# Regrouping the levels of a chunked scan inside a two-mixer encoder layer

## The chip, the cores and the metric

The kernel runs on one core of a Trainium2 chip. The metric is the device time of one execution in microseconds. Before the change three runs gave 1809.49, 1810.12 and 1810.22 us; the median is 1810.12.

## The reference: what is computed

One encoder layer over 1024 positions of width 1024, in float32. A normalised input is projected once onto 8192 columns, and two mixers run on them. The first is a convolution module. The second, which the change concerns, is a gated linear recurrence in both directions with 8 heads of width 128:

```python
a = jnp.cumsum(lfb, axis=2)
diff = a[:, :, :, None, :] - a[:, :, None, :, :]
decay = jnp.where(tril, jnp.exp(jnp.minimum(diff, 0.0)), 0.0)
scores = jnp.einsum("bhtk,bhsk,bhtsk->bhts", qb, kb, decay)
o = (jnp.einsum("bhts,bhsv->bhtv", scores, vb)
     + jnp.einsum("bhtk,bhkv->bhtv", qb * jnp.exp(a), state))
```

A score between positions t and s is a sum over key channels in which each channel is damped by the product of the forget gates that lie between s and t. The two directions are summed, normalised per head, gated by a third projection and projected back. The gated sum of both mixers goes through an output projection and a residual, and a gated feed-forward block with a short convolution and a last normalisation follow.

## The kernel before, in words

Large products are made from float32 values split into a rounded high part and a remainder, so that one product is three matmuls (`mm3`, lines 147 to 149: `mm<-hx,wp` in the profile). ScalarE rounds, VectorE subtracts (`split`, line 123). These are the dense work. It is cut into units by `yield`; most units are two steps of k, six matmuls of 512 columns. `Stream.fill(n)` runs n units and carries fractions over.

TensorE's instructions keep the order in which the program writes them. The other engines are ordered by a planner, which may bring an instruction forward as soon as its inputs and its buffer are there. A tile's buffers rotate: a new one waits until the last reader of the old one is done. In PSUM the scan uses `sc` (2 banks), `tr` (2) and `ob` (1); `mm` (3) belongs to the dense work.

The scan works through 16 half heads: 8 heads, each in two halves of 512 positions. One half head has four chunks of 128 positions. The damping within a chunk is not formed as a product over pairs of positions. Instead the scan doubles a block size h = 1, 2, 4, ... 64: at level h the scores between two neighbouring blocks of h positions are one product of keys, damped to the edge between the blocks, and queries, damped from it. After each level `double` (line 1111, its products on line 1052) multiplies keys `kG`, queries `qF` and block totals `tb` by the totals of the neighbours, so that they fit the next level.

- `scan_inputs` loads queries and gates and forms keys and forget factors on ScalarE, with a clip on VectorE.
- `scan_base` makes the diagonal (line 1138, two products per block, one for each direction) and levels 1, 2 and 4 in one `sc` bank, in 5 steps. Each level is 16 matmuls of 128 rows by 32 columns, four per chunk, that sit in different column groups of the array (`level`, line 1103). Their stationary operand is a page `A`, into which `key_blocks` (ScalarE, line 1083) has copied the keys so that the keys of a left and a right block stand side by side; the moving operand is a strided view of `qF`. Masks then pick the valid scores of each level into `D` (line 1153).
- `scan_levels` does levels 8 and 16 in the same way, each with an `ob` bank of its own (masks on lines 1187 and 1189), then 32 and 64 as plain blocks (`blocks`, line 1167) in an `sc` bank that is first zeroed by a matmul of zeros `none` (line 1182). It ends by copying everything to `S`.
- `scan_states` transposes the keys through two `tr` banks (line 1203), copies them (`kT`, line 1205) and multiplies them with the values (line 1212; `ob` for one direction, `sc` for the other). VectorE chains the forward states `Sf` out of `ob` (line 1220).
- `outputs` (with `scan_outputs`), one head later: it chains the backward states, then makes the output of each half in `ob` (line 1253), copies and squares it on ScalarE (1255, 1258), normalises it (1272), and turns each half back through a `tr` bank (1279), out of which VectorE reads (1281).

These parts are woven by `between`, called at every `yield` of `scan_levels` and `scan_states`. One call is a *place*: `FILL` = 1.3 units of dense work, one step of the next half head's base, and one step of the previous head's outputs (`pending`). There are 4 places from the levels and 3 from the states, 7 per half head and 14 per head; 7 x 1.3 = 9.1 units per half head. The base has 5 steps, the outputs have 8.

In one half head TensorE thus meets, each with dense work ahead of it: level 8; level 16; the next base's diagonal and level 1, then `none`, blocks of 32 and the transpose of the values (line 1353); level 2 and blocks of 64; level 4 and one key transpose; the other key transpose; the state products. The first base is made ahead of the loop, with 6 units and then 3 units after each of its steps.

Of the kernel before, what the change touches and what calls it, by code (L numbers as in the profile page):

```python
# [10 lines left out]
F32 = mybir.dt.float32  # L11
# [35 lines left out]
def tile_hybrid_encoder(  # L47
# [54 lines left out]
    def page(pool, tag, bufs, dt=F32):  # L102
        return pool.tile([P, H], dt, tag=tag, name=nm(tag), bufs=bufs)
# [973 lines left out]
    def pairs(t, h, other=H):  # L1077

        return view(t, 0, [[other + h, 2], [2 * h, H // (2 * h)], [1, h]])

    def key_blocks(kG, h):
        A_t = page(hp, "A", 3)
        A.copy(pairs(A_t, h, 0), pairs(kG, h))  # L1083
        return A_t

    def slot(b, n):
        return b[:, n * P : (n + 1) * P]
# [7 lines left out]
    def each():  # L1095
        for c in range(4):
            for g in range(0, P, 32):
                yield c * P + g, slice(g, g + 32), slice(32 * c, 32 * c + 32)

    def level(b, A_t, qF, h):  # L1100

        for at, g, o in each():
            T.matmul(  # L1103
                b[g, o].rearrange("p (b x e) -> p b x e", x=2, e=h),
                A_t[:, at : at + 32],
                view(qF, at, [[2 * h, 16 // h], [H + h, 2], [1, h]]),
                start=True,
                stop=True,
            )

    def double(kG, qF, tb, h, to=None):
# [3 lines left out]
        tt(pairs(qF, h), pairs(qF, h), view(tb, nb + 1, [[-(nb + 1), 2], [2, n], [0, h]]))  # L1115
        if to is None:
            tn = hp.tile([P, 2, n], F32, tag=f"tb{h}", name=nm("tb"), bufs=2)
            to = view(tn, 0, [[n, 2], [1, n]])
        else:
            tn = None  # L1120
        tt(to, view(tb, 0, [[nb, 2], [2, n]]), view(tb, 1, [[nb, 2], [2, n]]))
        return tn

    def scan_base(ins):


        q, f, kG, ks = ins
        qF = hp.tile([P, 2, H], F32, tag="qF", name=nm("qF"), bufs=4)
        D_t = hp.tile([P, 4, 32], F32, tag="D", name=nm("D"), bufs=3)
        for d in range(2):  # L1130
            V.tensor_scalar(kG[:, d, :], kG[:, d, :], ks[:, d : d + 1], None, op0=ALU.mult)
        A_t = key_blocks(kG, 1)
        tt(qF, view(q, 0, [[0, 2], [1, H]]), view(f, H, [[-H, 2], [1, H]]))
        yield
        b = bank("sc")
        for at, g, o in each():
            for d in range(2):
                T.matmul(
                    slot(b, 3)[g, o],
                    kG[:, d, at : at + 32],  # L1140
                    q[:, at : at + 32],
                    start=d == 0,
                    stop=d == 1,
                )
        tb = f
        for n, h in enumerate((1, 2, 4)):
            level(slot(b, n), A_t, qF, h)
            tb = double(kG, qF, tb, h)
            A_t = key_blocks(kG, 2 * h)
            yield  # L1150
        A.copy(D_t, near(slot(b, 2)))
        for n, m in ((0, m_1), (1, m_2), (3, m_d)):
            V.copy_predicated(D_t, over(m), near(slot(b, n)))
        yield qF, kG, A_t, tb, D_t

    def scan_levels(base, S_t, Tt):


        qF, kG, A_t, tb, D_t = base

        def blocks(b, h):

            for c in range(0, H, P):
                for s0 in range(0, P, h):
                    t0 = s0 ^ h
                    d = s0 // h % 2
                    T.matmul(  # L1167
                        b[s0 : s0 + h, c + t0 : c + t0 + h],
                        kG[:, d, c + s0 : c + s0 + h],
                        qF[:, 1 - d, c + t0 : c + t0 + h],  # L1170
                        start=True,
                        stop=True,
                    )

        for h in (8, 16, 32, 64):
            if h < 32:
                b = bank("ob")
                level(slot(b, 0), A_t, qF, h)
            else:
                if h == 32:  # L1180
                    b = bank("sc")
                    T.matmul(b, none[:, :P], none, start=True, stop=True)
                blocks(b, h)
            tb = double(kG, qF, tb, h, view(Tt, 0, [[4, 2], [1, 4]]) if h == 64 else None)
            if h == 8:
                A_t = key_blocks(kG, 16)
                V.copy_predicated(D_t, over(m_8), near(slot(b, 0)))
            elif h == 16:
                V.copy_predicated(D_t, over(m_16), near(slot(b, 0)))
            elif h == 64:  # L1190
                A.copy(S_t, c4(b))
                for g in range(0, P, 32):
                    A.copy(S_t[g : g + 32, :, g : g + 32], D_t[g : g + 32])
            yield

    def scan_states(i, kG, v, Tt, Sf, Sb):

        half = i % 2
        kTs = []
        for d in range(2):  # L1200
            b = bank("tr")
            for c in range(4):
                T.transpose(b[:, c * P : (c + 1) * P], kG[:, d, c * P : (c + 1) * P], ident)
            kT = page(hp, "kT", 2)
            A.copy(kT, b)
            kTs.append(kT)
            yield
        for d in range(2):
            u = bank("sc" if d else "ob")
            for c in range(4):  # L1210
                sl = slice(c * P, (c + 1) * P)
                T.matmul(u[:, sl], kTs[d][:, sl], v[:, c, :], start=True, stop=True)
            u4 = c4(u)
            if d == 0:
                for c in range(4 if half == 0 else 3):
                    nx = Sf[half][:, c + 1, :] if c < 3 else Sf[1][:, 0, :]
                    if half == 0 and c == 0:
                        V.tensor_copy(nx, u4[:, 0, :])
                    else:
                        V.scalar_tensor_tensor(  # L1220
                            nx,
                            Sf[half][:, c, :],
                            Tt[:, half, 0, c : c + 1],
                            u4[:, c, :],
                            op0=ALU.mult,
                            op1=ALU.add,
                        )
# [102 lines left out]
    for h in range(NH):  # L1330
        Tt = hp.tile([P, 2, 2, 4], F32, tag="Tt", name=nm("Tt"), bufs=3)
        Sf = [hp.tile([P, 4, DK], F32, tag="st", name=nm("Sf"), bufs=4) for _ in range(2)]
        Sb = [hp.tile([P, 4, DK], F32, tag="st", name=nm("Sb"), bufs=4) for _ in range(2)]
        kept = []
        for half in range(2):
            i = 2 * h + half
            base = cur.result()
            ahead = Base(ins) if i + 1 < NI else None
            ins = scan_inputs(i + 2) if i + 2 < NI else None

            def between(fill):
                dense.fill(fill)
                if ahead is not None:
                    ahead.step(BASE_STEPS)
                pending.fill(1)

            S_t = hp.tile([P, 4, P], F32, tag="S", name=nm("S"), bufs=3)
            vl = load(d_v[h][half])
            for n, _ in enumerate(scan_levels(base, S_t, Tt[:, half])):
                if n == 2:  # L1350
                    b = bank("tr")
                    for c in range(4):
                        T.transpose(b[:, c * P : (c + 1) * P], vl[:, c * P : (c + 1) * P], ident)
# [407 lines left out]
```

## Time and profile before

| | |
|---|---|
| median of 3 runs | 1810.12 us |
| profiled execution | 1807.26 us, span 1805.5 us |
| TensorE busy | 1757.3 us, 97% |
| VectorE busy | 1213.0 us, 67% |
| ScalarE busy | 804.1 us, 45% |
| granted TensorE clock, mean | 0.993 |

In the profile PE is TensorE's matmuls and PEld its weight loads, DVE is VectorE, ACT ScalarE, POOL GpSimd. A group's row has line, engine, operation, output and inputs by the program's names, shapes and count; behind the first bar the busy time and the mean duration of one in nanoseconds; behind the second the idle time of the engine just ahead of the group and what ended it. A float32 matmul that is written once in the code leaves two records, except for transposes. A row of waits has the waiting instruction, what released it, the sum in microseconds, how often, and the longest. In rows in order of time the columns are start and duration in microseconds, then engine, line, operation, names, shapes and the count that was merged into the row.

### The profile page before, as it was taken

What the parts mean: (1) busy time and instruction counts of PE and PEld (TensorE: products, weight loads), DVE (VectorE), ACT (ScalarE), POOL (GpSimd) and SP (SyncE); (2) the same over time, 40 slices, a digit from 0 to 9 for tenths busy, and PEclk for the clock granted to TensorE, in tenths of its full rate; (3) what the DMA queues carried; (4) which work ended last, traced back from release to release, by engine and by line L of the source; (5) the groups of instructions that cost most, each with busy time, mean ns of one, the idle gap of its engine ahead of it and who ended that gap; (6) DMA issues with size and microseconds to landing.
All of it is one profiled execution on the core that took longest, in us unless ns stands there. A gap on an engine that the chain in (4) does not pass through costs nothing.

```text
span 1805.5 us, 30702 instructions
## 1 busy us (share of the span) xinstructions
PE 1757.3 (97%) x12150; PEld 1433.9 (79%) x12150; DVE 1213.0 (67%) x1813; ACT 804.1 (45%) x1534; POOL 152.2 (8%) x165
## 2 busy tenths in 40 slices
PE   8989999999999999999989999999999999999997
PEld 6878877888877778877878888878888888888885
DVE  4599999657577777777545666766766766545355
ACT  6344332335466566756552245434434434422123
POOL 1201111000000000000000002011111111000000
PEclk9999999999999999999999999999999999999999
DMA  8658878746652333335358666576776765534233
GB/s 279 215 153 187 190 174 187 203 146 199 209 177 95 120 107 117 118 101 177 112 171 236 200 205 207 142 152 144 147 158 147 151 152 129 161 97 128 82 93 135
DMA packets 321270, 284.48 MB, mean 158 GB/s; under 512 B 14942, under 2 KB 242022, under 8 KB 321126
## 3 DMA queue, kind: packets, MB, share of 16 engines
q1 hardware_dynamic: 279958, 250.01, 44.0%
q0 software_dynamic: 41168, 32.51, 12.8%
q8 instruction: 95, 1.56, 0.3%
q14 instruction: 49, 0.40, 0.1%
HBM read 189.40 MB, written 76.81 MB: 147 GB/s over the span
## 4 chain that ended last, share of the span: by engine, by line
PE 72%; DVE 9%; DMA 7%; ACT 5%; issue 4%; POOL 1%; SPq 1%; POOLq 0%; ACTq 0%; DVEq 0%
PE mm L147 17%; PE mm L149 16%; PE mm L148 16%; PE sc L147 3%; PE sc L149 3%; PE sc L148 3%; DVE acc L956 2%; PE ob L1253 2%; DVE wp L123 2%; PE tr L147 2%; PE tr L149 2%; PE tr L148 2%; DMA ev<-d_ga 1%; PE sc L1103 1%; DMA wr<-in_w_in_dram 1%
## 5 line engine op out<-in xcount | busy, mean ns | idle before, releaser
L147 PE MATMUL mm<-hx,wp 128*128 128x512 f32 x1144 | 463.0, 405 | 9.3 <-DVE ev L718 4.9
L149 PE MATMUL mm<-hx,wp 128*128 128x512 f32 x1144 | 449.9, 393 | 2.1 <-DVE wp L123 2.0
L148 PE MATMUL mm<-hx,wp 128*128 128x512 f32 x1144 | 449.0, 392 | 0.0
L123 ACT CAST wp<-wr 128x1024 fp32r<-128x1024 f32 (+2 forms) x171 | 162.0, 948 | 342.9 <-PE mm L148 258.3
L147 PEld LDWEIGHTS mm<-hx,wp 128*128 128x128 f32 x1144 | 216.6, 189 | 56.1 <-DVE ev L718 7.4
L149 PEld LDWEIGHTS mm<-hx,wp 128*128 128x128 f32 x1144 | 216.3, 189 | 50.6 <-DVE wp L123 3.8
L148 PEld LDWEIGHTS mm<-hx,wp 128*128 128x128 f32 x1144 | 216.7, 189 | 41.3 <-issue 0.2
L123 DVE TENSOR_TENSOR wp<-wr,wp 128x1024 fp32r<-128x1024 f32 (+2 forms) x169 | 186.1, 1102 | 86.0 <-ACT wp L123 85.0
L956 DVE SCALAR_TENSOR_TENSOR acc<-gl,v_b,acc 128x1024 f32<-128x1024 f32 x120 | 149.6, 1284 | 0.4
L1083 ACT COPY A<-kG 128x512 f32<-128x512 f32 x80 | 51.1, 643 | 73.2 <-DVE kG L1052 70.4
L1612 DVE TENSOR_TENSOR xr<-mm,xr 128x512 f32<-128x512 f32 x48 | 33.2, 691 | 73.1 <-PE mm L149 73.1
L367 ACT COPY su<-mm 128x512 f32<-128x512 f32 x82 | 47.5, 579 | 71.6 <-PE mm L149 70.6
L1052 DVE TENSOR_TENSOR kG<-kG,tb 128x512 f32<-128x512 f32 x96 | 66.2, 690 | 18.6 <-PE sc L1167 9.6
L1052 DVE TENSOR_TENSOR qF<-qF,tb 128x512 f32<-128x512 f32 x96 | 66.0, 688 | 13.9 <-PE sc L1103 9.9
L123 ACT CAST wq<-sw 128x1024 fp32r<-128x1024 f32 x41 | 43.1, 1050 | 64.4 <-PE mm L148 25.2
L1461 DVE SCALAR_TENSOR_TENSOR tm<-gp,v_a,tm 128x512 f32<-128x512 f32 x88 | 66.0, 750 | 2.0
L147 PE MATMUL mm<-hy,wp 128*128 128x512 f32 x164 | 64.6, 394 | 1.4 <-ACT su L367 1.4
L147 PE MATMUL sc<-hy,wq 128*128 128x512 f32 x164 | 64.7, 394 | 0.0
L148 PE MATMUL mm<-hy,wp 128*128 128x512 f32 x164 | 64.3, 392 | 0.0
L149 PE MATMUL sc<-hy,wq 128*128 128x512 f32 x164 | 64.2, 391 | 0.0
L147 PE MATMUL tr<-hx,wp 128*128 128x512 f32 x164 | 64.0, 390 | 0.0
L149 PE MATMUL tr<-hx,wp 128*128 128x512 f32 x164 | 63.9, 389 | 0.0
(350 smaller groups left out, 3433.4 us busy)
## 6 DMA issues: line engine op xcount, KB each, us to landing
wr<-in_w_in_dram SPq DMA_DIRECT2D x56, 512.0 KB, 4.6
wr<-in_ffn_w_up_dram SPq DMA_DIRECT2D x24, 512.0 KB, 4.9
sw<-in_ffn_w_up_dram SPq DMA_DIRECT2D x44, 256.0 KB, 3.6
d_g<-ft SPq DMA_DIRECT2D x44, 256.0 KB, 2.4
sw<-in_ffn_w_up_dram POOLq DMA_DIRECT2D x20, 512.0 KB, 8.0
sw<-in_w_in_dram SPq DMA_DIRECT2D x38, 256.0 KB, 3.6
d_z<-ev SPq DMA_DIRECT2D x32, 256.0 KB, 3.6
zi<-d_z SPq DMA_DIRECT2D x32, 256.0 KB, 3.1
```

The costliest lines, as they stand in the source:

```text
L123: parts = A.copy(hi, src), eng.tensor_tensor(lo, src, hi.bitcast(F32), op=ALU.subtract)
L147: T.matmul(acc, whi[:, k, :], ahi, start=first, stop=False, skip_group_check=again)
L148: T.matmul(acc, whi[:, k, :], alo, start=False, stop=False, skip_group_check=again)
L149: T.matmul(acc, wlo[:, k, :], ahi, start=False, stop=last, skip_group_check=again)
L367: A.copy(t, acc)
L956: V.scalar_tensor_tensor(acc, g[:, k : k + S], tap(k), acc, op0=ALU.mult, op1=ALU.add)
L1052: V.tensor_tensor(o, a, b, op=op)
L1083: A.copy(pairs(A_t, h, 0), pairs(kG, h))
L1103: T.matmul(b[g, o].rearrange("p (b x e) -> p b x e", x=2, e=h), A_t[:, at : at + 32], view(qF, at, [[2 * h, 16 // h], [H + h, 2], [1, h]]) ...
L1253: T.matmul(o[:, sl], l, r, start=(n == 0), stop=(n == len(terms) - 1))
L1461: V.scalar_tensor_tensor(c, g[:, o + k : o + k + H], vec("fdw", k * NF + j), c, op0=ALU.mult, op1=ALU.add,)
L1612: V.tensor_tensor(xr[i][half], acc, xr[i][half], op=ALU.add)
```

## The change: what it does

- **Places.** `scan_levels` has three places (8 with 16; 32; 64) and `scan_states` two (both key transposes; the products), so five per half head and ten per head. `FILL` is 1.82, which again makes 9.1 units per half head. `BASE_STEPS` stays 1.
- **The batch.** Diagonal and levels 1, 2 and 4 run in one go at the base's third step. Steps 1 and 2 prepare all their operands: `woven` copies keys and, newly, queries into pages `A` (8 buffers instead of 3), so that `level` reads a plain row of 32 from both. Only level 16 still reads `qF` through a view.
- **The diagonal.** Keys of both directions are added on VectorE (`k_d`), so that one product per block replaces two.
- **Queries of level 1.** The 1024-wide product of `q` and `f` becomes two of 512: one goes straight into the woven page `Q1`, one into the odd places of `qF`.
- **Doubling 8** moves from `scan_levels` into the base's fourth step. `double` is cut into `double_keys`, `double_queries` and `totals`; the totals of h below 8 have one buffer instead of two.
- **Levels 8 and 16** share one `ob` bank, and their two masks are applied together.
- **`none`** is 128 by 32 instead of 128 by 512, and 16 small matmuls zero only the diagonal blocks of 32 that the levels 32 and 64 leave unwritten.

Copies into `A` per half head go from five (keys for 1, 2, 4, 8, 16) to eight (keys for these five, queries for 2, 4, 8). The masks stay five.

```diff
-FILL = 1.3
+FILL = 1.82
-    none = hp.tile([P, H], mybir.dt.bfloat16, name="none")
+    none = hp.tile([P, 32], mybir.dt.bfloat16, name="none")
...
-    def key_blocks(kG, h):
-        A_t = page(hp, "A", 3)
-        A.copy(pairs(A_t, h, 0), pairs(kG, h))
-        return A_t
+    def woven(t, h):
+
+        t_h = page(hp, "A", 8)
+        A.copy(pairs(t_h, h, 0), pairs(t, h))
+        return t_h
...
-    def level(b, A_t, qF, h):
-
+    def level(b, A_t, Q_t):
         for at, g, o in each():
-            T.matmul(
-                b[g, o].rearrange("p (b x e) -> p b x e", x=2, e=h),
-                A_t[:, at : at + 32],
-                view(qF, at, [[2 * h, 16 // h], [H + h, 2], [1, h]]),
-                start=True,
-                stop=True,
-            )
+            T.matmul(b[g, o], A_t[:, at : at + 32], Q_t(at), start=True, stop=True)
...
-            tn = hp.tile([P, 2, n], F32, tag=f"tb{h}", name=nm("tb"), bufs=2)
+            tn = hp.tile([P, 2, n], F32, tag=f"tb{h}", name=nm("tb"), bufs=1 if h < 8 else 2)
...
-        A_t = key_blocks(kG, 1)
-        tt(qF, view(q, 0, [[0, 2], [1, H]]), view(f, H, [[-H, 2], [1, H]]))
+        k_d, Q1 = page(hp, "A", 8), page(hp, "A", 8)
+        tt(k_d, kG[:, 0, :], kG[:, 1, :], ALU.add)
+        A1 = woven(kG, 1)
+        odd = H // 2
+        tt(
+            pairs(Q1, 1, 0),
+            view(q, 0, [[1, 2], [2, odd], [1, 1]]),
+            view(f, H, [[1 - H, 2], [2, odd], [1, 1]]),
+        )
+        tt(
+            view(qF, 1, [[H - 1, 2], [2, odd]]),
+            view(q, 1, [[-1, 2], [2, odd]]),
+            view(f, H + 1, [[-(H + 1), 2], [2, odd]]),
+        )
+        double_keys(kG, f, 1)
+        double_queries(qF, pairs(Q1, 1, 0), f, 1)
+        tb = totals(f, 1)
+        yield
+        A2, Q2 = woven(kG, 2), woven(qF, 2)
+        double_keys(kG, tb, 2)
+        double_queries(qF, pairs(qF, 2), tb, 2)
+        tb = totals(tb, 2)
+        A4, Q4 = woven(kG, 4), woven(qF, 4)
         yield
         b = bank("sc")
-        for at, g, o in each():
-            for d in range(2):
-                T.matmul(
-                    slot(b, 3)[g, o],
-                    kG[:, d, at : at + 32],
-                    q[:, at : at + 32],
-                    start=d == 0,
-                    stop=d == 1,
-                )
-        tb = f
-        for n, h in enumerate((1, 2, 4)):
-            level(slot(b, n), A_t, qF, h)
-            tb = double(kG, qF, tb, h)
-            A_t = key_blocks(kG, 2 * h)
-            yield
-        A.copy(D_t, near(slot(b, 2)))
-        for n, m in ((0, m_1), (1, m_2), (3, m_d)):
+        for n, (k_t, q_t) in enumerate(((k_d, q), (A1, Q1), (A2, Q2), (A4, Q4))):
+            level(slot(b, n), k_t, row(q_t))
+        double_keys(kG, tb, 4)
+        double_queries(qF, pairs(qF, 4), tb, 4)
+        tb = totals(tb, 4)
+        A8, Q8 = woven(kG, 8), woven(qF, 8)
+        yield
+        A.copy(D_t, near(slot(b, 3)))
+        for n, m in enumerate((m_d, m_1, m_2)):
             V.copy_predicated(D_t, over(m), near(slot(b, n)))
-        yield qF, kG, A_t, tb, D_t
+        double_keys(kG, tb, 8)
+        double_queries(qF, pairs(qF, 8), tb, 8)
+        tb = totals(tb, 8)
+        A16 = woven(kG, 16)
+        yield
+        yield qF, kG, tb, D_t, A8, Q8, A16
...
+        b = bank("ob")
+        level(slot(b, 0), A8, row(Q8))
+        level(slot(b, 1), A16, lambda at: view(qF, at, [[H + 16, 2], [1, 16]]))
+        tb = double(tb, 16)
+        for n, m in enumerate((m_8, m_16)):
+            V.copy_predicated(D_t, over(m), near(slot(b, n)))
+        yield
+        b = bank("sc")
+        for at, g, _ in each():
+            T.matmul(b[g, at : at + 32], none, none, start=True, stop=True)
+        blocks(b, 32)
+        tb = double(tb, 32)
+        yield
+        blocks(b, 64)
+        double(tb, 64, view(Tt, 0, [[4, 2], [1, 4]]))
+        A.copy(S_t, c4(b))
+        for g in range(0, P, 32):
+            A.copy(S_t[g : g + 32, :, g : g + 32], D_t[g : g + 32])
+        yield
...
             A.copy(kT, b)
             kTs.append(kT)
-            yield
+        yield
...
-                if n == 2:
+                if n == 1:
                     b = bank("tr")
```

More of the change, by code (lines that the diff above doesn't have):

```diff
@@ L1156, in scan_levels @@
+        for n, m in enumerate((m_d, m_1, m_2)):
+            V.copy_predicated(D_t, over(m), near(slot(b, n)))
+        double_keys(kG, tb, 8)
[4 more added lines that the diff above has]
+        yield qF, kG, tb, D_t, A8, Q8, A16
     def scan_levels(base, S_t, Tt):
-        qF, kG, A_t, tb, D_t = base
+        qF, kG, tb, D_t, A8, Q8, A16 = base
         def blocks(b, h):
@@ L1173, in blocks, with double @@
                     )
[L1175 to L1193, printed above, removed]
-            yield
+        def double(tb, h, to=None):
+            double_keys(kG, tb, h)
+            double_queries(qF, pairs(qF, h), tb, h)
+            return totals(tb, h, to)
+        b = bank("ob")
[17 more added lines that the diff above has]
+        yield
     def scan_states(i, kG, v, Tt, Sf, Sb):
@@ L1206, in scan_states @@
             kTs.append(kT)
-            yield
+        yield
         for d in range(2):
```

13 lines of the change are left out of this document (9 added, 4 removed).

## The prediction

> **What bounds the kernel.** I read the page first, for the bound and the profiled execution's own length.
>
> ```profile
> span 1805.5 us, 30702 instructions
> PE 1757.3 (97%) x12150; PEld 1433.9 (79%) x12150; DVE 1213.0 (67%) x1813; ACT 804.1 (45%) x1534; POOL 152.2 (8%) x165
> ```
>
> TensorE is busy for 97% of the span, so an edit counts by what it takes from or adds to TensorE's own queue. The profiled execution took 1807.26 us, 2.9 under the median of the runs (1810.12); I make the sum as a difference and put it on the median. Next, the busy time by stretch: the one that holds all scan instructions, and inside it one whose clock is lower.
>
> ```profile
> core 0: us, PE busy (x) PEld busy (x) DVE busy (x) ACT busy (x) POOL busy (x), PEclk, DMA share, GB/s
> 600.00:640.00 40.00, 37.76 (x641) 30.64 (x628) 29.28 (x63) 22.67 (x56) 1.14 (x2) 0.96 0.32 104
> ...
> 500.00:905.00 405.00, 393.89 (x6117) 317.74 (x6116) 294.83 (x611) 254.53 (x591) 12.83 (x14) 0.99 0.38 123
> ```
>
> The scan stretch leaves TensorE only 11.1 us idle in 405 (405.00 - 393.89). VectorE is free for 110 us of it, ScalarE for 150. Then the groups of that stretch, with TensorE's small matmuls:
>
> ```profile
> L1103 PE MATMUL sc<-qF,A 128*32 128x32 f32 x1536 | 25.1, 204 | 2.9 <-issue 2.7
> L1138 PE MATMUL sc<-q,kG 128*32 128x32 f32 x1024 | 14.0, 202 | 0.0
> L1182 PE MATMUL sc<-none 128*128 128x512 bf16 x16 | 6.2, 385 | 0.0
> ```
>
> There are 16 half heads. 1536 records are 96 for each: three levels of 16 matmuls in `sc`, each written matmul giving two records. The diagonal has 1024/16 = 64, for 32 written ones. A mean of 204 ns is a latency: four column groups overlap, so costs must be read from start to start. One half head in order of time on TensorE (start, duration, count at the end):
>
> ```profile
> 700.77 0.40 PE L148 MATMUL mm<-hx,wp 128*128 128x512 f32 x1
> 701.00 0.40 PE L149 MATMUL mm<-hx,wp 128*128 128x512 f32 x1
> 701.33 0.76 PE L1138 MATMUL sc<-q,kG 128*32 128x32 f32 x58
> ...
> 702.46 0.39 PE L1182 MATMUL sc<-none 128*128 128x512 bf16 x1
> 702.78 0.46 PE L1167 MATMUL sc<-qF,kG 128*32 128x32 f32 x32
> 703.17 0.65 PE L1353 MATMUL tr<-ident,tm 128*128 128x128 f32 x4
> 703.58 0.48 PE L147 MATMUL mm<-hx,wp 128*128 128x512 f32 x1
> 703.89 0.39 PE L148 MATMUL mm<-hx,wp 128*128 128x512 f32 x1
> ...
> 705.15 0.46 PE L1103 MATMUL sc<-qF,A 128*32 128x32 f32 x32
> 705.54 0.69 PE L1167 MATMUL sc<-qF,kG 128*64 128x64 f32 x16
> 706.15 0.50 PE L147 MATMUL mm<-hx,wp 128*128 128x512 f32 x1
> ```
>
> From start to start: a dense matmul 0.23 us (700.77 to 701.00); diagonal with level 1, 1.13; `none`, 0.32; blocks of 32, 0.39; level 2, 0.39; blocks of 64, 0.61. Levels 4, 8 and 16 have level 2's form: 0.39 each. The column-tiled work is 1.13 + 0.32 + 0.39 + 0.61 + 4 x 0.39 = 4.01 us per half head. Two edges show: from dense into tiled work 0.33 instead of 0.23, so +0.10; and the first dense matmul after a cluster 0.31 instead of 0.23, +0.08.
>
> **The change, part by part.**
>
> *TensorE's matmuls.* The diagonal drops from 64 records to 32 and joins levels 1, 2 and 4 in one batch of 128. Level 2 alone is 32 in 0.39, diagonal with level 1 is 96 in 1.13: about 11.8 ns a record. Scaling the longer, 128 x 1.13/96 = 1.51 us. The short one gives a lower end: its 32 records last 0.46, of which the last one's latency is 0.20, so 31 steps take 0.26, 8.4 ns each, and 0.13 of the 0.39 is paid at the end; paid once for the batch that is 128 x 0.0084 + 0.13 = 1.20. I take 1.42, nearer the long cluster, since the batch is longer still. Before, these parts were 1.13 + 0.39 + 0.39 = 1.91: **0.49 saved**. Levels 8 and 16 together: 64 records, 64 x 11.8 ns = 0.76 against 0.78: 0.02 saved.
>
> *`none`.* One 512-column matmul, 0.32, becomes 16 of 32 columns. At 11.8 ns or less they are 0.19, with 0.13 as lower end (8.4 ns) and 0.74 as upper end, if they ran at the pace of the 16 records of the blocks of 64 (0.61) with an edge of 0.13 on top. I take 0.17, because their form is the tiled one: **0.15 saved**.
>
> The Trainium skill ("TensorE: Matmul & The Clock Gate", the section "Wait — 56ns, not 53.3ns?") says that start to start never falls below about 25 ns however narrow a matmul is. By that, 16 matmuls are an estimated 0.40 us, and this edit costs 0.08 x 16 = 1.3 us instead of gaining 2.4. The 32 records in 0.39 us above speak against it for column-tiled work.
>
> *Places.* Seven become five, with the same dense work (7 x 1.3 = 5 x 1.82 = 9.1 units per half head). Two restarts fewer, 2 x 0.08, and entries into tiled work go from five (8, 16, diagonal, 2, 4) to four (8+16, `none`, blocks of 64, batch), 0.10: **0.26 saved**.
>
> Sum on TensorE: 0.49 + 0.02 + 0.15 + 0.26 = 0.92 us x 16 = **-14.7 us**. With the ends of the batch (1.20 to 1.51) it is -18.2 to -13.3.
>
> *VectorE and ScalarE.* The rows that price the new work:
>
> ```profile
> L1052 DVE TENSOR_TENSOR kG<-kG,tb 128x512 f32<-128x512 f32 x96 | 66.2, 690 | 18.6 <-PE sc L1167 9.6 <-ACT A L1083 8.2
> L1083 ACT COPY A<-kG 128x512 f32<-128x512 f32 x80 | 51.1, 643 | 73.2 <-DVE kG L1052 70.4 <-PE sc L1103 2.4
> L1052 DVE TENSOR_TENSOR qF<-q,f 128x1024 f32<-128x1024 f32 x16 | 19.5, 1221 | 0.1
> ```
>
> The 1024-wide query product becomes two of 512 and the key sum is added: 3 x 0.69 - 1.22 = +0.85 us, 13.6 us over 16. Copies per half head go from 5 to 8: 3 x 0.643 x 16 = +30.9 us of ScalarE. Both cost nothing if they fall into the 110 and 150 idle us; without that cover they are those 13.6 and 30.9. No DMA is added or moved past another; SP's and POOL's queues keep their work.
>
> *Waits that go.* Those of the scan on TensorE and around it:
>
> ```profile
> DVE kG L1131 <- ACT kG L1071: 21.3, 13, 4.1
> ...
> PE ob L1103 <- DVE D L1187: 4.9, 7, 2.0
> ...
> PE sc L1103 <- issue: 2.7, 2, 2.1
> ...
> PE ob L1103 <- DVE Sf L1220: 2.1, 5, 0.9
> ...
> PE sc L1212 <- ACT kT L1205: 0.9, 2, 0.7
> ```
>
> Level 16 waits 4.9 us for VectorE to read level 8 out of the only `ob` bank; sharing the bank removes that. Level 8's wait for the forward states (2.1) shrinks, as the fill ahead of it grows from 1.3 to 1.82 units of six dense matmuls (0.7 us): I count 1.1 of it. **-6 us**; next late is still the forward-state chain.
>
> *Waits that come.* (1) The previous head's last turn of outputs (fill 8 of `pending`) now comes at the third place of the second half, straight ahead of both key transposes. `tr` has two banks, so the second key transpose takes the bank of that turn and must wait for VectorE to read it. A like pair, TensorE's turn and the read:
>
> ```profile
> 694.96 0.60 PE L1279 MATMUL tr<-ident,tm 128*128 128x128 f32 x4
> 695.58 0.46 PE L1103 MATMUL ob<-qF,A 128*32 128x32 f32 x32
> ```
> ```profile
> 695.59 0.75 DVE L1281 SCALAR_TENSOR_TENSOR ev<-tr,v_a,og 128x512 f32<-128x512 f32 x1
> ```
>
> The read ends 1.38 us after the turn starts (695.59 + 0.75 - 694.96); the turn and the first key transpose cover 2 x 0.41 of it. At least 0.56, and up to 1.2 more when VectorE is inside its longest operation. At 0.85, for seven heads: **+6 us** (4 to 12). (2) Both key copies now run in one fill instead of two; in a first half they stand behind the output copy and squares. Row L1212 is 0.9 today; I take **+2 us** (0 to 8). (3) The first batch needs four ready pairs, not one; only the 12 units of dense work ahead of it cover: **+1 us** (0 to 3). (4) `A` has 8 pages for 10 a half head: the copies for 4 wait for level 8+16, three places ahead of the batch, hidden by three fills of 1.82 x 6 x 0.23 = 2.5 us; uncovered, two copies, 1.3 us.
>
> **Sum:** -14.7 - 6 + 6 + 2 + 1 = -11.7 us, so 1798.4 on the median; I say **1798**. The ends: -18.2 - 7 + 4 = -21 with the best of each, -13.3 - 5 + 12 + 8 + 3 = +5 with the worst, and `none` at 0.74 would add (0.74 - 0.17) x 16 = 9.
>
> **The rivals.**
>
> *A. The batch comes late (slower).* Before, the first tiled work of a base needed two key scalings, one product and one copy; now it needs ten VectorE operations and the copies up to 4. If VectorE does them in program order, they share the first three places with other work: base steps 1 and 2 (two scalings in 1.00, below, and 8 x 0.69, 6.5 us), doublings 16 and 32 (4 x 0.69 = 2.8) and a dense split (1024 wide, like the 1.22), 10.5, and then two copies, 1.3. TensorE gives three fills of 2.5 and clusters of 0.76, 0.17 + 0.39 + 0.41 and 0.61, 9.8 us. Late by 2.0 us per half head: +32 on the forecast, about 1830. It decides at 11.7/16 = 0.73 us per half head. Against it:
>
> ```profile
> 713.17 1.00 DVE L1131 TENSOR_SCALAR kG<-kG,kscale 128x512 f32<-128x512 f32 x2 [0.98 <-ACT kG L1071]
> ```
>
> VectorE scales those keys while TensorE is still in the half head before; with the 21.3 us wait above it shows that base work starts as soon as its inputs exist. A long stall also costs clock here: after an idle of 2.08 us the next dense matmul took 0.77 instead of 0.48, and the 40 us around it show 0.96.
>
> ```profile
> 602.79 0.44 PE L1103 MATMUL sc<-qF,A 128*32 128x32 f32 x19 [2.08 <-issue]
> ...
> 604.49 0.77 PE L147 MATMUL mm<-hx,wp 128*128 128x512 f32 x1
> ```
>
> The Trainium skill (same page, "What's actually happening") has the clock halve after an idle window of about 3.4 us. By that rule stalls of 2.0 us would mostly not pay it; this trace paid after 2.08.
>
> *B. Instruction supply.* That 2.08 us stall is inside diagonal and level 1, with no engine behind it ("issue"). The batch, 128 matmuls and as many weight loads, is as dense and a third longer. One such stall, with some 1.4 us of slow matmuls behind it, in every third half head is 5 x 3.5 = 17 us, less the 2.7 there are: about 1812, no change.
>
> *C. Nothing new is waited for.* VectorE, no longer tied to the levels' reads of `qF`, is free when the turn lands, and the batch runs at its fast end: -18.2 - 6 = -24 at most, about 1786.
>
> **Chances.** The forecast (1792 to 1806) 0.53, C 0.22, B 0.11, A 0.14. A measurement of this kernel tells about 0.2%, 3.6 us. B splits over "same"; A is slower. Faster 0.77, same 0.09, slower 0.14. The range 1783 to 1814 takes in C and B.
>
> **What would show it.** Right: L1138 gone, batches of 128 records in about 1.4 us, no wait on L1187 ahead of a level, 16 `none` records in under 0.2. Wrong: TensorE waiting on an `A` copy at the batch (A); "issue" in the batch (B); for the new waits, a key transpose waiting on L1281's operation in seven places, and state matmuls on kT.

## The result, and the profile after

The changed kernel takes 1785.8 us (median of 4 runs, 1783.6 to 1788.7) beside 1809.8 for the kernel before (median of 4). The ratio is 0.9872, with a 95% interval of 0.9852 to 0.9893: 24 us, or 1.3%, faster. The profiled execution took 1786.31 us against 1807.26.

The page after:

```profile
span 1784.5 us, 30262 instructions
PE 1733.0 (97%) x11878; PEld 1424.5 (80%) x11878; DVE 1213.2 (68%) x1845; ACT 827.8 (46%) x1582; POOL 152.1 (9%) x165
```

TensorE is still busy for 97% of the span; its busy time fell by 24.3 us (1757.3 - 1733.0). ScalarE's rose by 23.7. VectorE's stayed, although it has 32 more instructions.

One half head after, TensorE in order of time:

```profile
695.17 0.46 PE L1103 MATMUL sc<-q,A 128*32 128x32 f32 x32
695.45 1.07 PE L1103 MATMUL sc<-A,A 128*32 128x32 f32 x96
696.45 0.66 PE L1302 MATMUL tr<-ident,tm 128*128 128x128 f32 x4
...
704.40 0.39 PE L149 MATMUL mm<-hx,wp 128*128 128x512 f32 x1
704.72 0.46 PE L1103 MATMUL ob<-A,A 128*32 128x32 f32 x32
704.99 0.49 PE L1103 MATMUL ob<-qF,A 128*32 128x32 f32 x32
705.41 0.50 PE L147 MATMUL mm<-hx,wp 128*128 128x512 f32 x1
705.74 0.39 PE L148 MATMUL mm<-hx,wp 128*128 128x512 f32 x1
...
708.37 0.28 PE L1208 MATMUL sc<-none 128*32 128x32 bf16 x16
708.48 0.47 PE L1186 MATMUL sc<-qF,kG 128*32 128x32 f32 x32
```

The batch of 128 records takes 1.28 us from start to start (695.17 to 696.45), levels 8 and 16 together 0.69 (704.72 to 705.41), the zeros 0.11 (708.37 to 708.48). Diagonal with levels 1, 2 and 4 took 1.91 before, levels 8 and 16 0.78, the zeros 0.32. That is 0.93 us per half head, 15 in all. The edges are there as before: 0.32 from the last dense matmul into a tiled one, 0.33 for the first dense one after it.

Now TensorE's waits in the scan stretch after (waiter, releaser, sum, times, longest):

```profile
PE sc L1186 <- DVE qF L1052: 4.2, 4, 1.8
...
PE tr L1226 <- DVE ev L1304: 3.9, 3, 2.0
...
PE tr L1226 <- ACT kT L1228: 2.7, 4, 0.7
...
PE sc L1103 <- ACT A L1084: 1.9, 2, 1.6
```

The two `ob` waits of before, 7.0 us, are gone, and so are the 2.7 us of "issue"; these four lines, 12.7 us together, have come.

The span alone doesn't say how the 24 us divide. I took the start times of all TensorE records from the 1980th to the 3300th dense matmul in both traces, which is the stretch with the scan and the same dense work, and gave each interval to the kind of the record that begins it, but every interval into or out of dense work to the dense row. An interval that is more than 130 ns over the median of its kind of transition holds a wait, and what it has over the median is the wait. In four kernels (before, seven places, fill last, before with the cuts) half or more of one kind of transition waited, so that its median holds a wait; there the undisturbed interval of that kind stands for the median. Before the change it is the transition from a transpose to a level, 203 ns instead of 432. Dense intervals at half speed are set apart.

| us | before | after | difference |
|---|---|---|---|
| diagonal and levels | 38.9 | 29.3 | -9.6 |
| zeros | 5.0 | 1.9 | -3.1 |
| blocks of 32 and 64 | 13.6 | 13.7 | +0.1 |
| transposes, state products, outputs | 94.1 | 94.1 | 0.0 |
| dense matmuls with their edges | 329.6 | 320.4 | -9.2 |
| waits | 19.0 | 19.0 | 0.0 |
| half speed | 3.1 | 1.4 | -1.7 |
| stretch | 503.6 | 479.8 | -23.8 |

So the whole gain lies in this stretch (the rest of the profiled execution is 2.8 us longer: the span fell by 21.0). Some 13 us are less tiled work, 9 are dense work with its edges, not quite 2 are less half speed, and waits gave nothing: as much came as went.

### The profile page after: what moved, and what is told of

Its sections match the earlier page's. It is cut to its first block, busy times and chain, and to the rows that moved or that the text cites. A ratio compares the mean times of both kernels' runs of the same rounds, so it can differ in the third digit from the quotient of the medians.

```text
span 1784.5 us, 30262 instructions
## 1 busy us (share of the span) xinstructions
PE 1733.0 (97%) x11878; PEld 1424.5 (80%) x11878; DVE 1213.2 (68%) x1845; ACT 827.8 (46%) x1582; POOL 152.1 (9%) x165
## 4 chain that ended last, share of the span: by engine, by line
PE 72%; DMA 10%; DVE 9%; issue 4%; ACT 3%; POOL 1%; SPq 0%; POOLq 0%; ACTq 0%; DVEq 0%
PE mm L147 17%; PE mm L148 17%; PE mm L149 17%; PE sc L147 3%; PE sc L149 3%; PE sc L148 3%; DMA sw<-in_w_in_dram 3%; DVE acc L956 2%; PE ob L1276 2%; DMA wr<-in_w_in_dram 2%; DMA wr<-wr 2%; DVE wp L123 2%; PE tr L147 1%; PE tr L148 1%; PE tr L149 1%
## 5 line engine op out<-in xcount | busy, mean ns | idle before, releaser
L147 PEld LDWEIGHTS mm<-hx,wp 128*128 128x128 f32 x1144 | 216.1, 189 | 60.1 <-DVE ev L718 10.6
L147 PE MATMUL tr<-hx,wp 128*128 128x512 f32 x164 | 63.9, 390 | 0.0
L149 PE MATMUL tr<-hx,wp 128*128 128x512 f32 x164 | 63.8, 389 | 0.0
L148 PE MATMUL tr<-hx,wp 128*128 128x512 f32 x164 | 63.8, 389 | 0.0
```

The lines of the kernel that those rows point to most:

```text
L147: T.matmul(acc, whi[:, k, :], ahi, start=first, stop=False, skip_group_check=again)
L148: T.matmul(acc, whi[:, k, :], alo, start=False, stop=False, skip_group_check=again)
L149: T.matmul(acc, wlo[:, k, :], ahi, start=False, stop=last, skip_group_check=again)
```

## The experiments

Each kernel was timed in three rounds beside the kernel before. I compare ratios and turn their differences into us on 1809.8. A ratio has an interval of about 0.002 either way, 4 us, and a difference of two ratios about 5. The last column is from the same count as in the table above, where the kernel before has 19.0.

| kernel | ratio to before | against | us | waits in the stretch |
|---|---|---|---|---|
| changed kernel | 0.9872 | before | -24 | 19.0 |
| zeros by one matmul | 0.9871 | changed | 0 | 17.7 |
| diagonal twice | 0.9903 | changed | +6 | 21.5 |
| seven places | 0.9929 | changed | +10 | 21.5 |
| outputs first | 0.9904 | changed | +6 | 21.0 |
| before, five places | 1.0169 | before | +31 | 45.5 |
| two `ob` banks | 0.9971 | changed | +18 | 35.8 |
| strided rows | 0.9879 | changed | +1 | 18.0 |
| fill last | 0.9871 | changed | 0 | 22.1 |
| turn in `mm` | 0.9838 | changed | -6 | 11.6 |
| turn one place later | 0.9821 | changed | -9 | 10.9 |
| no masks | 0.9883 | changed | +2 | 19.4 |
| before with the cuts | 0.9936 | before | -12 | 18.2 |

My theory at the start was that the gain is tiled work taken off TensorE. The rival was that it comes from the regrouping: fewer and longer fills.

**Zeros by one matmul.**

```diff
-    none = hp.tile([P, 32], mybir.dt.bfloat16, name="none")
+    none = hp.tile([P, H], mybir.dt.bfloat16, name="none")
...
-        for at, g, _ in each():
-            T.matmul(b[g, at : at + 32], none, none, start=True, stop=True)
+        T.matmul(b, none[:, :P], none, start=True, stop=True)
```

> The changed kernel (1785.8 us) with one edit undone: the bank is zeroed by one matmul of 512 columns again, in place of 16 of 32 columns. Theory (the gain is column-tiled work taken off TensorE): the 16 small ones took 0.11 us from start to start, the wide one 0.32, so +0.21 x 16 = +3.4 us, 1789. Rival (the small ones cost as much as the wide one, by a floor of 25 ns each): no change, 1786.

The runs show no difference (0.9849 to 0.9892). The expected 3.4 us compared the steps alone, 0.11 with 0.32 us, and left out that the sixteen small ones now pay the entry into tiled work, which with the wide matmul lies behind it. From the last dense matmul to the first block of 32 the trace has 0.55 us here (709.05 to 709.60) and 0.43 in the changed kernel (708.05 to 708.48): 0.12 x 16 = 1.9 us, which is less than these runs can tell.

**Diagonal twice.**

```diff
-        for n, (k_t, q_t) in enumerate(((k_d, q), (A1, Q1), (A2, Q2), (A4, Q4))):
+        for at, g, o in each():
+            for d in range(2):
+                T.matmul(slot(b, 0)[g, o], k_d[:, at : at + 32], q[:, at : at + 32], start=d == 0, stop=d == 1)
-            level(slot(b, n), k_t, row(q_t))
+        for n, (k_t, q_t) in enumerate(((A1, Q1), (A2, Q2), (A4, Q4))):
+            level(slot(b, n + 1), k_t, row(q_t))
```

> The changed kernel with the diagonal as two products per block again (the added keys are used twice, so the diagonal counts double; the work has the old count of matmuls). Theory: 32 more records at the 9 ns that the batch shows, 0.29 x 16 = +4.6 us, 1790. Rival (the matmuls hide in a wait behind them, and the gain came from the order of the work): no change, 1786.

It was 6 us slower, near the theory. In the trace the diagonal's intervals rose from 4.4 to 10.5 us. Matmuls taken off TensorE here are time.

**The cuts on the kernel before.** The counterpart, in the old order:

```diff
-    none = hp.tile([P, H], mybir.dt.bfloat16, name="none")
+    none = hp.tile([P, 32], mybir.dt.bfloat16, name="none")
...
+        k_d = page(hp, "kd", 2)
+        tt(k_d, kG[:, 0, :], kG[:, 1, :], ALU.add)
...
-            for d in range(2):
-                T.matmul(slot(b, 3)[g, o], kG[:, d, at : at + 32], q[:, at : at + 32], start=d == 0, stop=d == 1)
+            T.matmul(slot(b, 3)[g, o], k_d[:, at : at + 32], q[:, at : at + 32], start=True, stop=True)
...
-                    T.matmul(b, none[:, :P], none, start=True, stop=True)
+                    for at, g, _ in each():
+                        T.matmul(b[g, at : at + 32], none, none, start=True, stop=True)
```

> The kernel before with the TensorE cuts alone: the keys of both directions added and one product per block of the diagonal, and 16 small matmuls of zeros; seven places, levels and banks as before. Theory (this work is on TensorE's path): 32 records fewer at 9.9 ns and 0.21 us of zeros, 0.53 x 16 = -8.5 us against the kernel before, 1801. Rival (the sum of keys, 11 us on VectorE ahead of the diagonal, is waited for): within 3 us of the kernel before.

It gained 12 us (0.9911 to 0.9961), 3 more than expected. Its row of the diagonal has half the records of before (1024):

```profile
L1139 PE MATMUL sc<-q,kd 128*32 128x32 f32 x512 | 7.3, 199 | 0.0
```

In the count diagonal and levels fell from 38.9 to 31.6 and the zeros from 5.0 to 1.9; the waits stayed (19.0, 18.2). These two cuts, which need none of the regrouping, are about half of the gain.

**Seven places.**

```diff
-FILL = 1.82
+FILL = 1.3
...
         level(slot(b, 0), A8, row(Q8))
+        yield
...
             kTs.append(kT)
-        yield
+            yield
...
-                if n == 1:
+                if n == 2:
```

> The changed kernel with seven places of 1.3 units again: a place between level 8 and level 16 (one bank still) and one between the two key transposes. Theory: two more restarts and one more entry, +0.26 x 16 = +4.2 us, but the last turn of outputs falls into another place, so the key transposes' 6.6 us of waits go: -2.4 in sum, 1783. Rival (fewer, longer fills are where most of the 24 us come from; the dense matmuls lost 10.5 us between the two traces): +10 us, 1796.

The rival's number came, +10 us where I expected -2, though 10 of 24 isn't most of the gain. Dense matmuls with their edges rose from 320.4 to 326.8 us in the count, 6.4 where I had put 4.2. The wait at the key transposes did go, but the sum of the waits rose (19.0 to 21.5). TensorE's waits of this version, in the scan stretch:

```profile
PE ob L1277 <- DVE D L1205: 3.2, 4, 1.3
PE ob L1103 <- DVE Sf L1244: 3.1, 5, 1.1
```

Outputs now meet the masked copy of the `ob` bank, and level 8 the forward states, as before the change.

**The five places on the kernel before.**

```diff
-FILL = 1.3
+FILL = 1.82
...
-            yield
+            if h != 8:
+                yield
...
             kTs.append(kT)
-            yield
+        yield
...
-                if n == 2:
+                if n == 1:
```

> The kernel before with the places alone regrouped: five places of 1.82 units (levels 8 and 16 in one place but still with a bank each, both key transposes in one), nothing else. Theory (fewer restarts and entries are worth about 7.4 us, as the seven-place version of the changed kernel showed in its trace, but level 16 now stands right behind VectorE's read of level 8 in the one ob bank, some 0.5 us in each of 16 half heads, and the key transposes wait for the turn, 7.8 us): about +8, 1818. Rival (the regrouping of places alone carries the gain): 1800 or less.

It was 31 us slower (1.0151 to 1.0188), far beyond the 8 expected. Put into the kernel before by itself, the regrouping loses. Dense matmuls with their edges do fall in the count, from 329.6 to about 323 us, but the waits rise from 19.0 to 45.5 and the time at half speed by some 5 to 7 us. TensorE's waits say why:

```profile
PE ob L1103 <- DVE D L1187: 29.9, 16, 4.4
```

Level 16 waits 1.9 us for the `ob` bank in each half head, since VectorE reads level 8 when its queue comes to it, not when level 8 is done. I had counted the read's own time, 0.5. One such wait:

```profile
703.22 0.46 PE L1103 MATMUL ob<-qF,A 128*32 128x32 f32 x32
...
704.45 0.49 DVE L1131 TENSOR_SCALAR kG<-kG,kscale 128x512 f32<-128x512 f32 x1 [3.03 <-ACT kG L1071]
704.85 0.69 DVE L1052 TENSOR_TENSOR qF<-qF,tb 128x512 f32<-128x512 f32 x1
705.45 0.29 DVE L1187 COPY_PREDICATED D<-m,ob 128x128 f32<-128x128 uint8 x1
...
705.89 0.66 PE L1103 MATMUL ob<-qF,A 128*32 128x32 f32 x32 [2.21 <-DVE D L1187]
```

Level 8 is done at 703.68 (703.22 + 0.46). VectorE has nothing to do until 704.45, because the instruction that stands next in its queue waits for keys from ScalarE, and it reads level 8 only at 705.45.

**Two `ob` banks** in the changed kernel, the same wait put back alone:

```diff
         level(slot(b, 0), A8, row(Q8))
-        level(slot(b, 1), A16, lambda at: view(qF, at, [[H + 16, 2], [1, 16]]))
+        V.copy_predicated(D_t, over(m_8), near(slot(b, 0)))
+        b = bank("ob")
+        level(slot(b, 0), A16, lambda at: view(qF, at, [[H + 16, 2], [1, 16]]))
         tb = double(tb, 16)
-        for n, m in enumerate((m_8, m_16)):
-            V.copy_predicated(D_t, over(m), near(slot(b, n)))
+        V.copy_predicated(D_t, over(m_16), near(slot(b, 0)))
```

> The changed kernel with a bank each for levels 8 and 16 in the one place, so that level 16 waits for VectorE's masked read of level 8. Theory (the shared bank is needed once both levels stand in one place): the wait is at least the read of 0.3 us and its hand-over on both sides, 0.5 to 1.5 us in 16 half heads, +8 to +24 us, 1794 to 1810. Rival (other waits shrink by as much, since something else is late next): under +4 us.

```profile
PE ob L1103 <- DVE D L1201: 18.9, 16, 3.5
```

It cost 18 us, inside the theory's range. The shared bank is what lets five places pay.

**Strided rows.**

```diff
-        return lambda at: t[:, at : at + 32]
+        return lambda at: view(t, at // 2, [[2, 32]])
```

> The changed kernel with the moving operand of levels 1, 2, 4, 8 and of the diagonal read with a step of two elements instead of as a plain row (it reads other queries, so the scores are others; count and size of the work are the same). Theory (the plain row is not what made the levels faster; the batch's 9 ns a record is the pace of the array's column groups): no change, 1786. Rival (strided rows were the 11.8 ns a record of diagonal with level 1): 2.6 ns x 160 records x 16 = +6.7 us, 1793.

No difference that the runs can tell (0.9864 to 0.9894), and the levels took 29.5 us against 29.3. Weaving the queries into plain rows doesn't make the matmuls faster. VectorE's products that write `qF` waited 15.5 us for levels on TensorE before (11.7 on those in `sc`, 3.8 on those in `ob`) and 1.0 after, since most levels now read a copy. But its products that write pages `A` now wait 14.5 us for the batch, and that the copies gain time by themselves isn't shown.

The next four ask about the new wait at the key transposes. In the changed kernel TensorE and VectorE stood like this around it, at its longest:

```profile
741.70 0.66 PE L1302 MATMUL tr<-ident,tm 128*128 128x128 f32 x4
...
742.19 0.60 PE L1226 MATMUL tr<-ident,kG 128*128 128x128 f32 x4
742.23 0.69 DVE L1052 TENSOR_TENSOR A<-kG 128x512 f32<-128x512 f32 x1
742.83 0.69 DVE L1052 TENSOR_TENSOR qF<-qF,tb 128x512 f32<-128x512 f32 x1
...
743.43 0.69 DVE L1052 TENSOR_TENSOR kG<-kG,tb 128x512 f32<-128x512 f32 x1
...
744.03 0.75 DVE L1304 SCALAR_TENSOR_TENSOR ev<-tr,v_a,og 128x512 f32<-128x512 f32 x1
...
744.84 0.66 PE L1226 MATMUL tr<-ident,kG 128*128 128x128 f32 x4 [2.05 <-DVE ev L1304]
```

The last turn of outputs is done at 742.36 (741.70 + 0.66), but three products stand ahead of its read in VectorE's queue. TensorE waits 2.05 us for 0.75 us of work. So it is in three of the seven heads, 3.9 us in all. In the other four the second key transpose starts before VectorE's read of the turn is over, so it can't have waited for that. It starts about 0.06 us after ScalarE's copy of the first one has ended, each time with a wait of 0.7 us:

```profile
697.58 0.58 ACT L1228 COPY kT<-tr 128x512 f32<-128x512 f32 x1
...
698.22 0.65 PE L1226 MATMUL tr<-ident,kG 128*128 128x128 f32 x4 [0.68 <-ACT kT L1228]
698.34 0.75 DVE L1304 SCALAR_TENSOR_TENSOR ev<-tr,v_a,og 128x512 f32<-128x512 f32 x1
```

The trace doesn't name the bank. I read it so: the turn (here at 696.45) holds one of the two `tr` banks, the first key transpose the other, and the second one waits for whichever of them it was given. The two runs below that take the turn out of the way bear this out, since both kinds of wait go.

**Outputs first.**

```diff
                 dense.fill(fill)
+                pending.fill(1)
                 if ahead is not None:
                     ahead.step(BASE_STEPS)
-                pending.fill(1)
```

> The changed kernel with the two steps at each place swapped: the previous head's outputs before the next base's step, so that the batch of 128 matmuls stands between the last turn of outputs and the key transposes. Theory: VectorE's read of that turn ends 1.4 us after the turn starts, the turn, the batch and the first key transposes take 0.5 + 1.3 + 0.4 = 2.2, so the wait of the second key transpose for it (3.9 us in the trace, 7.8 us of lost TensorE time with the wait for the key copies) goes: -5 to -7 us, 1780. Rival (the wait only moves, to the turn itself or to the state products): no change, 1786.

It was 6 us slower. The wait at the key transposes fell to 1.1 us (the second row), and another one came (the first):

```profile
PE ob L1103 <- DVE Sf L1243: 5.9, 6, 2.0
...
PE tr L1226 <- DVE ev L1304: 1.1, 2, 0.7
```

Level 8 waits for the forward states. One more part: a stall in the first batch here was followed by a stretch at half speed. From 510 to 525 us the profile has a granted clock of 0.77, where the changed kernel has 1.00; that is half speed for some 7 of the 15 us.

```profile
510.00:525.00 15.00, 12.66 (x165) 9.97 (x164) 13.50 (x29) 11.38 (x21) 0.00 (x0) 0.77 0.48 158
```

From this I took it that waits in this stretch only move, and that VectorE's fill sets them. The two runs below that take the turn out of the way refute the first part, and the one without masks speaks against the second.

**Fill last.**

```diff
-                dense.fill(fill)
                 if ahead is not None:
                     ahead.step(BASE_STEPS)
                 pending.fill(1)
+                dense.fill(fill)
```

> The changed kernel with the order at a place turned: base step, outputs, then the dense fill. The batch of 128 follows the blocks of 64 without dense work between them, and a whole fill (2.5 us) stands between the last turn of outputs and the key transposes. Theory: one entry into tiled work fewer (0.09 x 16 = 1.5 us), and the key transposes' wait (7.8 us) goes: -5 to -9, 1777 to 1781, a version better than both. Rival (as in the version with the outputs first: the wait moves, to level 8 behind the forward states or to the batch, which now comes a fill earlier): 1784 to 1792.

No gain: the rival. But most of what came in its place is of another kind. TensorE in order of time:

```profile
648.86 0.69 PE L1186 MATMUL sc<-qF,kG 128*64 128x64 f32 x16
649.48 0.46 PE L1103 MATMUL sc<-q,A 128*32 128x32 f32 x32
649.75 1.04 PE L1103 MATMUL sc<-A,A 128*32 128x32 f32 x92
653.25 0.26 PE L1103 MATMUL sc<-A,A 128*32 128x32 f32 x4 [2.46 <-issue]
...
653.85 0.71 PE L147 MATMUL mm<-hx,wp 128*128 128x512 f32 x1
```

With blocks of 64 straight ahead of the batch, TensorE stops 3 or 4 records before its end, with no engine behind it, twice (2.46 and 2.82 us). The 5 us from 651 on have a granted clock of 0.79. That is the stall of my rival B, in a version where more small matmuls follow one another. That instructions came late is my reading of it: in both stalls, and in the one of 2.08 us before the change, TensorE goes on about 1.5 us after a transfer of 16 KB in the trace's queue for instructions has ended, but no run varies that.

**Turn in `mm`.**

```diff
-            b = bank("tr")
+            b = bank("mm")
```

(in the last turn of `scan_outputs`)

> The changed kernel with the outputs' last turns written to an mm bank, so that the key transposes no longer share tr with them. Theory (waits of TensorE in this stretch hang on VectorE's and ScalarE's full queues; one that is taken away comes back in part at the next place): the 7.8 us at the key transposes go, about half comes back at levels, blocks or state products: -3 to -5 us against the changed kernel, 1781 to 1783. Rival 1 (the wait stands alone): -7 to -8, 1778. Rival 2 (all of it moves, as in the version with the outputs first): 1786.

It gained 6 us, and the waits fell from 19.0 to 11.6: nearly all of the wait, by both routes, went and little came back.

**Turn one place later.**

```diff
-            def between(fill):
+            def between(fill, turn=True):
...
-                pending.fill(1)
+                if turn:
+                    pending.fill(1)
...
-                between(FILL)
+                between(FILL, half == 0 or n != 2)
```

(the last line in the loop over `scan_levels`)

> The changed kernel with no output step at the third place of a second half, so that the last turn comes one place later, behind the key transposes. Theory (as for the turn in an mm bank): -3 to -5 us, 1781 to 1783. Rival 1: -7 to -8, 1778. Rival 2: the turn's read now stands on VectorE among the forward states, level 8 waits, 1786 or more.

It gained 9 us: the first rival, the wait stands alone. The ratio to the kernel before is 0.9821 (0.9799 to 0.9844), whose interval lies below that of the changed kernel: **this version, 1778.1 us, beats both.** All of TensorE's waits that the view lists from 500 to 935 us:

```profile
PE sc L1186 <- DVE qF L1052: 5.1, 4, 1.8
PE tr L1302 <- ACT tm L1295: 2.6, 2, 2.1
PE sc L1103 <- ACT A L1084: 0.9, 1, 0.9
PE ob L1276 <- ACT tm L1278: 0.7, 1, 0.7
```

No key transpose waits any more, and nothing waits on the forward states.

**No masks.**

```diff
-        for n, m in enumerate((m_d, m_1, m_2)):
-            V.copy_predicated(D_t, over(m), near(slot(b, n)))
```

> The changed kernel without the three masked copies of the batch (diagonal and levels 1 and 2 are left out of the scores), 3 x 0.30 x 16 = 14.4 us less on VectorE, nothing less on TensorE. Theory (TensorE's waits in the stretch, 19 us, hang on VectorE's queue at 77% busy): they shrink by a quarter to a half, -5 to -9 us, 1777 to 1781. Rival (VectorE has room, the waits are single collisions): under -2 us.

The 48 masked copies that are left out lasted 0.30 us each, but such a copy overlaps with its neighbour (the one at 744.70 in the changed kernel lasts 0.30 us and the next product starts at 744.89), and VectorE's busy time fell by 7.8 us only (1213.2 to 1205.4). Nothing is faster (0.9858 to 0.9908), and the waits are the same (19.4 us):

```profile
PE sc L1184 <- DVE qF L1052: 6.0, 7, 2.5
PE tr L1224 <- DVE ev L1302: 3.5, 3, 1.7
```

The forecast of my second theory, a quarter to a half less waiting, doesn't come. This takes only some 3% off VectorE's work in the stretch (294.7 to 285.7 us from 500 to 883 us), so by itself it is a weak test. Together with the rows of the five-places version of the kernel before, in which VectorE had nothing to do and TensorE still waited for it, it says that these waits hang on which instruction stands ahead of the awaited one in VectorE's queue more than on how full that queue is.

## Why the prediction was right in sign and range, and short in size

The forecast was 1798 in a range of 1783 to 1814, with 0.77 for faster. It is 1785.8, twice as far as the likeliest sum (-11.7, measured -24). It lies outside the 1792 to 1806 that had the chance of 0.53, and inside the range only because the range took in rival C. No single step failed; four sizes were off, all to the same side: the matmuls by 4 us, the waits by 3, the places by 2, and half speed, which the sum left out, by not quite 2. Step by step:

- **TensorE's matmuls** were right in kind and too small. The batch took 1.28 us (1.42 taken, 1.20 the lower end), levels 8 and 16 0.69 (0.76), the zeros 0.11 (0.17). The sum was 0.66 us per half head, measured 0.93: 15 us for 10.6. The row that misled was the long cluster of before: its slower pace wasn't one of long clusters. And two clusters in one save a way out, 0.13 us; the forecast had read these 0.13 off level 2, but took them into the batch's lower end alone and not into levels 8 and 16.
- **Places** were a little small. The sum had 0.26 us per half head, 4.2 in all. The count has 9.2 for dense matmuls with their edges, but 2.8 of these are ways out into dense work (8.9 us before, 6.1 after), which costs from start to start, and so the 0.93 above, mostly hold already. That leaves 6.4. My edges were of the right size (0.09 to 0.10 each). What I didn't count is that the second to fourth dense matmuls after a cluster are each some 5 ns slow. A way out, from the last small matmul to the first dense one, is 0.13 to 0.15 us where it is 0.03 from a full-array one. Undoing the places cost 6.4 us in that row of the trace, ways out included, and 10 in the runs, give or take 5.
- **Waits that go** were right: the two `ob` waits went, 7.0 us for 6 forecast. Giving each level its own bank in one place costs 18 us, so the five places are only worth something together with the shared bank.
- **Waits that come** were right in place, and near in sum; the cause was right in three heads of seven. The second key transpose waits in all seven heads, because the turn holds one of the two `tr` banks, and TensorE loses 7.8 us there in the count for 6 forecast. But the sign that I had named, a wait on VectorE's read of the turn in seven places, shows in three. There the read ended 1.4 to 3.1 us after the turn's start (at the longest 744.78 - 741.70), where the pair of before had 1.38. In the other four it is ScalarE's copy of the first key transpose that is waited for. The state products, for which I had 2, don't wait. In their place blocks of 32 and 64 wait 4.2 us for doubled queries, which I had not seen. The first batch waited 1.9 us for its copies, 1 forecast. With the "issue" stall and some smaller waits gone too, all waits together are what they were, 19.0 us, where the forecast had 3 more.
- **VectorE and ScalarE at nothing** was right: ScalarE's 23.7 us more (30.9 forecast for the 48 copies, whose row has 30.8) and VectorE's extra work are hidden. VectorE's busy time didn't rise by the 13.6 that I had put as its most, but by 0.2.

Of the rivals, C had the number (1786) for the wrong reason: it put the work at -18 and the waits at -6, and the work was worth about -22 (the first, second and fifth rows of the table), half speed not quite -2 and the waits nothing. That its number came out is luck. A didn't happen: beyond the first, no batch waits for its copies. B didn't happen here, but the fill-last version shows that a stall of its kind can happen in the batch.

What stays open is the share of the zeros, about 2 us by the traces and too small for the runs, and why diagonal and level 1 were slower per record before: 11.8 ns with the way out (0.14 us) and 10.4 without it, now 10.0 and 9.1. The strided reads aren't the cause.

## What to carry to other kernels

When small matmuls are woven into dense ones, count each visit's way in, way out and restart, a third of a microsecond here, beside the matmuls; but merge two visits only together with the buffers that keep the second from waiting for another engine's read of the first. A wait for a bank costs what stands ahead of the read in the reader's queue, so move the awaited instruction or give it another bank before taking work off the reader: one output step moved by one place gained 9 us, 48 masked copies left out gained nothing.

## What the runs showed of the hardware that I had not expected

- Sixteen bf16 matmuls of 32 columns took 0.11 us from start to start, 7 ns each. This is far below the floor of about 25 ns that the Trainium skill gives ("TensorE: Matmul & The Clock Gate", "Wait — 56ns, not 53.3ns?"); for column-tiled matmuls the trace decides.
- In the fill-last version TensorE stood still for 2.46 and 2.82 us, with no engine behind it, after some 140 matmuls and as many weight loads in 1.9 us (648.86 to 649.75 + 1.04), both times 3 to 4 matmuls before the end of the batch.
- After the idle time of 2.46 us TensorE ran at half speed for some 3.4 us (dense matmuls 0.43 us apart instead of 0.23, from 653.85 to about 657); once, in the version with the outputs first, for some 7. After the longer one of 2.82 us, and after the 2.05 us at a key transpose of the changed kernel, it did not. So the length of one idle time doesn't settle it here.
